# A three-mixer layer on one core: head pairs with a 64-row third product, shuffles issued by GpSimd, 13 warm-ups and a new weave

## The chip, the cores and the metric

The kernel runs on one core of a Trainium2 chip. The metric is the device time of one launch in microseconds. "TensorE" (PE), "VectorE" (DVE), "ScalarE" (ACT), "GpSimd" (POOL) and "SyncE" (SP) are the core's engines; each takes its own instructions in a fixed order and waits on semaphores. SyncE only issues transfers (DMAs); GpSimd can issue them too.

## What is computed

One layer on a sequence of T = 512 tokens with D = 1024 channels: a norm, one input projection, three mixers side by side, and an output projection with the residual.

```python
h = rmsnorm(x, norm_g[l])
proj = jnp.matmul(h, w_in[l])
(gq, gk, gv, glr, gg, su, sg, nq, nkv, ngl, ng) = jnp.split(proj, IN_SPLITS, axis=-1)
y_gla = gla_mixer(gq, gk, gv, glr, gg, ...)
y_s5 = s5_mixer(su, sg, ...)
y_nsa = nsa_mixer(nq, nkv, ngl, ng, ...)
x = x + jnp.matmul(jnp.concatenate([y_gla, y_s5, y_nsa], axis=-1), w_out[l])
```

GLA is a gated linear attention with 4 heads. S5 is a complex state-space scan in 16 groups of 64 states: chunks of 8 tokens, a scan over the 64 chunk states (xs), and a convolution inside a chunk with a table tt. NSA is an attention with 8 heads of 64 channels in two KV groups of 4 heads. It has three branches per head, mixed by gates: compressed keys, selected blocks and a window. For T = 512 the last two are both a causal softmax over all earlier tokens, each with its own keys and values:

```python
s_s = jnp.einsum('bqghd,bgqkld->bgqhkl', qb, k_g, preferred_element_type=f32)
p_s = masked_softmax(s_s.reshape(shp[:4] + (-1,)), m_s.reshape(B, G, Q_BLOCK, 1, -1)).reshape(shp)
o_s = jnp.einsum('bgqhkl,bgqkld->bqghd', p_s, v_g.astype(f32))
s_w = jnp.einsum('bqghd,bkgd->bgqhk', qb, kw, preferred_element_type=f32)
p_w = masked_softmax(s_w, m_w[None, None, :, None, :])
o_w = jnp.einsum('bgqhk,bkgd->bqghd', p_w, vw.astype(f32))
o = gb[..., 0:1] * o_c + gb[..., 1:2] * o_s + gb[..., 2:3] * o_w
```

## The kernel before

Inputs are fp32. A product that must be exact is made of three fp32r products: each operand is split into a high part hi and a low part lo = x - hi, and hi*hi, hi*lo and lo*hi are added in PSUM. ScalarE makes hi, VectorE makes lo (`load_part`, lines 224 to 226, for the weights: tiles wr, wh, wl; `split` for others). Weights of the input projection come in 12 groups of some 256 columns (su, qk, v, kv0, nq0, kv1, kv2, ng0, nq1, gg, sg, ng1), each in four parts, through a ring of six hi/lo buffers and three staging buffers wr.

The program is five streams, each a generator that yields at chosen points: p (projections), g (GLA), s (S5), n (NSA: compression and attention), o (output projection). The string ORDER (lines 43 to 48, "the weave") says which stream takes the next step. From the order in which the steps write their instructions, and from priorities, the framework sets each engine's fixed order. PSUM has eight banks: three "ps", three "pt" and two "pp"; the projections use pp.

The places that matter here:

- `start` sends nine warm-up matmuls (WARM) of 512 columns in bf16 ahead of the first real matmul, which waits for the first split of x (xh, xl). Then come the groups su and qk, the row norms and rbc. The input of S5, su, is written to DRAM (tile ud, two transfers) and read back reordered as u with eight transfers of 16 rows (line 353), all issued by SyncE.
- `gla_v` writes the values vv to DRAM (vd, line 393) and makes from them, with seven transfers, a second DRAM tile vp (line 395) in which the rows of each of seven levels stand together. `gla_intra` loads ve from vp.
- `cmp_blocks` projects kv0, scales into tm, and moves tm to aT by four transfers for each of two halves (line 943); VectorE adds positions from aT into bk (line 950).
- `s5_in` makes the tables gt, hb and kt on VectorE, writes kt and a zero block zz to DRAM (kd) and reads tt with eight transfers; `s5_scan` computes xs on VectorE. On TensorE the products "hb,xs" and "tt,u" use it.
- `attn_score` handles one head e of a head pair pr, for one block i of 128 query tokens. Keys up to the diagonal are n = 128(i+1). For i of 2 and 3 each branch has a bank of its own. The 128 rows of q hold q-hi and q-lo, those of kA[:, 0] hold k-hi twice and kA[:, 1] k-lo twice, so that two products give all four terms; the causal mask of the diagonal block is added by a third matmul of bf16 operands:

```python
mm(pb, q, kA[:, 0, br, :n], True, False)
mm(pb, q, kA[:, 1, br, :n], False, False)
mm(pb[:, n - 128:], identb, maskneg, False, True)
```

VectorE takes the row maximum, ScalarE the exponential with its sum, VectorE the reciprocal times the gate (dn), and GpSimd multiplies p by it (line 1155). `attn_out` transposes p on TensorE (line 1168), copies it out of PSUM to pT, and multiplies by the values kvr: each head's product uses 64 of the 128 columns, two heads side by side.

In the profile a matmul's tile shape stands ahead of its operands: 128*128 is the whole array, 128*64 half the columns, 64*128 half the rows.

Of the kernel before, what the change touches and what calls it, by code (L numbers as in the profile page):

```python
# [18 lines left out]
T = 512  # L19
# [16 lines left out]
for _n, _w in SMALL:  # L36
# [7 lines left out]
    "ppsgsgspppppsssspsssssgonspggsssgppgggppsgppsspgsppgppgngnsgggsnnnssspspppsggnggppppggssgggpsppggnnp"  # L44
    "gnsgpggpnpppgpgngngpggggggpgggggngggggggggggggggpppggnnnnnnpppnnnnnnnppnpnppppnnnnnnnnnpnnnppnnnnnnn"
    "nnpnnnnnnnppnnnnnnnnnnppnpppnpnnnnnnppnnnnnnnnonpppoooooooonooononnnoononnnooonnnnponnnnnnnnnnnnnnon"
    "nnoonnnnoooononnnnnooooonnnnooonnonnooooooonooooonooono"
)
WARM = 9
# [12 lines left out]
def kernel(ctx: ExitStack, tc: tile.TileContext, a: dict, out: bass.AP):  # L62
# [105 lines left out]
    identb = const.tile([128, 128], BF16, name="identb")  # L168
    maskneg = const.tile([128, 128], BF16, name="maskneg")
# [133 lines left out]
    def start():  # L303
# [29 lines left out]
        with tc.high_priority(offset=20 * BOOST):  # L333
            V.tensor_scalar(ms, ms, 1.0 / D, EPS, op0=OP.mult, op1=OP.add)
            rsqrt(rsc, ms)
            pr = bank()
            for i in range(NT):
                dg = al("dg", (128, 128))
                V.tensor_scalar(dg, ident, rsc[:, i:i + 1], None, op0=OP.mult)
                mm(pr[:, tok(i)], one, dg, True, True)  # L340
            V.tensor_copy(rbc, pr)
            ud = dram.tile([8, 256, NCH], F32, name="ud")
            for m in range(2):
                su = al("su", (128, LC, NCH))
                V.tensor_tensor(su, ps["su", m].rearrange("p (n j) -> p j n", j=LC),
                                rbc.rearrange("p (n j) -> p j n", j=LC), op=OP.mult)
                nc.sync.dma_start(out=ud[:, 128 * m:128 * m + 128].rearrange("j c n -> c j n"), in_=su)
            V.scalar_tensor_tensor(qT, ps["qk", 0], 32 ** -0.5, rbc, op0=OP.mult, op1=OP.mult)
            V.tensor_tensor(kT, ps["qk", 1], rbc, op=OP.mult)
        N["u"] = u = al("u", (128, 16, NCH), keep=True)  # L350
        for j in range(LC):
            jj = LC - 1 - j
            nc.sync.dma_start(out=u[16 * jj:16 * jj + 16], in_=ud[j].rearrange("(g c) n -> c g n", c=16))

    def consts():
# [22 lines left out]
        V.tensor_copy(identb, ident)  # L378
        V.tensor_copy(maskneg, nb)


    def gla_v():
# [9 lines left out]
        vp = dram.tile([7 * 256, 256], F32, name="vp")  # L392
# [4 lines left out]
        N["vp"] = vp  # L397
# [92 lines left out]
    def gla_intra():  # L490
        oT, vp, qT, kT = N["oT"], N["vp"], N["qT"], N["kT"]
        for lo, lv in ((-1, (0,)), (0, (1, 2)), (2, (3, 4)), (4, (5, 6))):
            with scope():
# [3 lines left out]
                for x, l in enumerate(lv):  # L497
# [6 lines left out]
                    nc.sync.dma_start(out=ve, in_=vp[l * 256:(l + 1) * 256].rearrange("(q p) e -> p q e", p=128))  # L504
# [166 lines left out]
    def s5_out_weights():  # L671
# [53 lines left out]
        nc.sync.dma_start(out=kd[0:7].rearrange("l c x -> (l c) x"), in_=zz)  # L725
# [228 lines left out]
    def cmp_mlp():  # L954
# [157 lines left out]
    def attn(gx):  # L1112
        units = [(i, pr, e) for i in (3, 2, 1, 0) for pr in range(2) for e in range(2)]
# [11 lines left out]
    def attn_score(gx, i, pr, e):  # L1125
        kA = N["kA"][gx]
        n = (i + 1) * 128
        h = gx * 4 + 2 * pr + e
        q = N[f"qA{gx}"][:, 2 * pr + e, tok(i)]
        dn = al("dn2", (128, 2), keep=True)  # L1130
        p = al("p", (128, 2, T), keep=True)
        with scope():
            nm = al("nm", (128, 2))
            if i >= 2:
                sv = []
                for br in range(2):
                    pb = bank("ps")[:, :n]
# [3 lines left out]
                    V.tensor_reduce(nm[:, br:br + 1], pb, axis=AX.X, op=OP.max, negate=True)  # L1141
                    sv.append(pb)
            else:
                pb = bank("ps")[:, :2 * n].rearrange("p (b t) -> p b t", b=2)
                mm(pb, q, kA[:, 0, :, :n], True, False)
                mm(pb, q, kA[:, 1, :, :n], False, False)
                mm(pb[:, :, n - 128:], identb, maskneg[:, None, :].to_broadcast([128, 2, 128]), False, True)
                V.tensor_reduce(nm, pb, axis=AX.X, op=OP.max, negate=True)
                sv = [pb[:, 0], pb[:, 1]]
            for br in range(2):  # L1150
                S.activation(p[:, br, :n], sv[br], AF.Exp, bias=nm[:, br:br + 1], accum_out=dn[:, br:br + 1])  # L1151
        V.reciprocal(dn, dn)
        V.tensor_tensor(dn, dn, gates[:, i, h * 3 + 1:h * 3 + 3], op=OP.mult)  # L1153
        for br in range(2):
            G.tensor_tensor(p[:, br, :n], p[:, br, :n], dn[:, br:br + 1].to_broadcast([128, n]), op=OP.mult)  # L1155
# [3 lines left out]
    def attn_out(gx, i, pr, e, live, x):  # L1159
        kvr = N["kvr"]  # L1160
        n = (i + 1) * 128
        p = live.pop(x)
        for br in range(2):
            live[e, br] = pt = al("pT", (128, T), keep=True)
            with scope():
                pb = bank("pt")
                for j in range(i + 1):
                    PE.transpose(pb[:, tok(j)], p[:, br, tok(j)], ident)  # L1168
                if cnt[0] % 2 == 0:
                    V.tensor_copy(pt[:, :n], pb[:, :n])  # L1170
                else:
                    S.activation(pt[:, :n], pb[:, :n], AF.Copy)  # L1172
# [9 lines left out]
        if i % 2:  # L1182
# [5 lines left out]
        for br in range(2):  # L1188
            for j in range(i + 1):
                for h2 in range(2):  # L1190
                    mm(o[64 * h2:64 * h2 + 64], kvr[br][:, j, 128 + gx * 64:192 + gx * 64],
                       live[h2, br][:, tok(j)], False, i % 2 == 0 and pr == 1 and br == 1 and j == i)
        for h2 in range(2):
            for br in range(2):
                fr(live.pop((h2, br)))
        yield
        if i % 2 == 0 and pr == 1:
# [21 lines left out]
def _prepare(inp):  # L1219
# [101 lines left out]
```

## Time and profile before

| | us |
|---|---|
| median of three runs | 366.1 (365.79 to 370.13) |
| profiled execution, whole time | 367.57 |
| its span from first to last instruction | 365.7 |
| TensorE busy | 341.3 (93%) |
| VectorE busy | 238.5 (65%) |
| ScalarE busy | 165.9 (45%) |
| GpSimd busy | 70.6 (19%) |
| mean granted TensorE clock | 0.977 of full |

Busy time of TensorE contains the time in which a matmul passes through the array beside the next one, so a matmul of 512 columns lasts 0.4 us though the next one starts 0.23 us after it. What a matmul costs is read from the distance of starts. Full clock is 2.4 GHz; the lower level is 1.2 GHz.

### The profile page before, as it was taken

To read this page: it belongs to the slowest core of one execution; us is meant where nothing else is said; L and a number is where in the kernel's file an instruction comes from. 1 tells how busy PE (TensorE), PEld (TensorE's weight loads), DVE (VectorE), ACT (ScalarE), POOL (GpSimd) and SP (SyncE) were. 2 spreads that over 40 slices of the span, in tenths; PEclk is the share of its full clock that TensorE was granted. 3 is DMA by queue.
4 is the path that set the end of the run, shared out by engine and by line. 5 is a ranking of instruction groups with operands and counts; after the bars stand their busy time and mean duration, and the time that the engine had idled before them with its cause. 6 is when DMAs were issued, how large, how long until landed. Compare 5 with 4: busy or idle time off the path is not lost.

```text
span 365.7 us, 6895 instructions
## 1 busy us (share of the span) xinstructions
PE 341.3 (93%) x2616; PEld 270.6 (74%) x2616; DVE 238.5 (65%) x528; ACT 165.9 (45%) x365; POOL 70.6 (19%) x92
## 2 busy tenths in 40 slices
PE   6999993989299999999999999999999898999996
PEld 3789983879177777987898777777764686777785
DVE  2847966779946467387736669647888837944332
ACT  3873541136244443453333766435876326743110
POOL 0000100000000000010100026733587117731100
PEclk9899999799789999999999999999999999999999
DMA  6996476424915355145204230001343112210122
GB/s 187 330 381 207 116 211 207 148 76 125 213 39 182 102 163 167 54 129 156 79 30 117 64 81 2 1 2 50 102 138 115 59 59 86 89 58 2 57 86 88
DMA packets 32843, 41.67 MB, mean 114 GB/s; under 512 B 7469, under 2 KB 22446, under 8 KB 32750
## 3 DMA queue, kind: packets, MB, share of 16 engines
q1 hardware_dynamic: 32810, 41.23, 37.6%
q8 instruction: 21, 0.34, 0.4%
q14 instruction: 12, 0.10, 0.1%
HBM read 35.14 MB, written 5.23 MB: 110 GB/s over the span
## 4 chain that ended last, share of the span: by engine, by line
PE 74%; DVE 11%; DMA 10%; issue 2%; SPq 1%; ACT 1%; DVEq 0%; ACTq 0%
PE pp L165 35%; PE pt L165 19%; PE ps L165 13%; PE pt L1168 5%; DMA aT<-tm 3%; DMA wor<-in_w_out_dram 2%; DMA vd<-vv 2%; DMA vp<-vd 1%; DMA w<-in_w_dram 1%; DMA xr<-in_xT_dram 1%; DVE wol L1071 1%; DVE wl L226 1%; DVE bk L950 1%; DVE h L691 1%; DVE hb L692 1%
## 5 line engine op out<-in xcount | busy, mean ns | idle before, releaser
L1155 POOL TENSOR_TENSOR p<-p,dn 128x512 f32<-128x512 f32 (+3 forms) x64 | 48.1, 775 | 41.1 <-DVE dn L1153 35.6
L165 PE MATMUL pp<-wh,xh 128*128 128x256 f32 (+2 forms) x160 | 47.6, 298 | 6.5 <-ACT qr L276 6.4
L226 DVE TENSOR_TENSOR wl<-wr,wh 128x512 fp32r<-128x512 f32 (+2 forms) x48 | 33.8, 707 | 25.7 <-ACT wh L225 25.6
L165 PE MATMUL pp<-wh,xl 128*128 128x256 f32 (+2 forms) x160 | 47.1, 295 | 0.0
L165 PE MATMUL pp<-wl,xh 128*128 128x256 f32 (+2 forms) x160 | 47.1, 295 | 0.0
L1151 ACT ACTIVATE p<-ps,nm 128x512 f32<-128x512 f32 (+3 forms) x64 | 33.2, 527 | 26.8 <-PE pt L1168 16.8
L225 ACT ACTIVATE wh<-wr 128x512 fp32r<-128x512 f32 (+2 forms) x48 | 30.4, 635 | 29.9 <-PE pp L165 11.8
L165 PEld LDWEIGHTS pp<-wh,xh 128*128 128x128 f32 x160 | 31.2, 195 | 8.7 <-ACT qr L276 6.8
L165 PE MATMUL pp<-xh,wh 128*128 128x512 f32 x80 | 32.3, 404 | 0.0
L165 PE MATMUL pp<-xh,wl 128*128 128x512 f32 x80 | 32.3, 405 | 0.0
L165 PEld LDWEIGHTS pp<-wl,xh 128*128 128x128 f32 x160 | 31.3, 195 | 1.3 <-issue 0.8
L165 PEld LDWEIGHTS pp<-wh,xl 128*128 128x128 f32 x160 | 31.2, 195 | 1.3 <-issue 0.8
L165 PE MATMUL pp<-xl,wh 128*128 128x512 f32 x80 | 32.0, 400 | 0.0
L1168 PE MATMUL pt<-ident,p 128*128 128x128 f32 x160 | 28.4, 282 | 3.3 <-DVE sc L1033 2.3
L165 PE MATMUL ps<-kA,qA 128*128 128x512 f32 (+2 forms) x96 | 29.7, 391 | 0.0
L165 PE MATMUL pt<-pT,kvr 128*64 128x128 f32 x320 | 29.4, 282 | 0.0
L1168 PEld LDWEIGHTS pt<-ident,p 128*128 128x128 f32 x160 | 18.5, 140 | 9.6 <-issue 6.0
L1141 DVE TENSOR_REDUCE nm<-ps 128x1 f32<-128x512 f32 (+1 forms) x32 | 19.4, 615 | 8.5 <-PE ps L165 8.4
L165 PEld LDWEIGHTS pt<-pT,kvr 128*64 128x64 f32 x320 | 19.9, 136 | 6.4 <-issue 3.1
L1170 DVE COPY pT<-pt 128x512 f32<-128x512 f32 (+3 forms) x32 | 15.4, 482 | 9.5 <-PE pt L1168 9.3
L1172 ACT ACTIVATE pT<-pt 128x512 f32<-128x512 f32 (+3 forms) x32 | 13.9, 434 | 16.8 <-PE pt L1168 16.8
L165 PEld LDWEIGHTS ps<-kA,qA 128*128 128x128 f32 x96 | 15.8, 191 | 3.6 <-issue 0.9
(386 smaller groups left out, 737.2 us busy)
## 6 DMA issues: line engine op xcount, KB each, us to landing
w<-in_w_dram SPq DMA_DIRECT2D x16, 256.0 KB
wor<-in_w_out_dram SPq DMA_DIRECT2D x16, 256.0 KB
xr<-in_xT_dram SPq DMA_DIRECT2D x8, 256.0 KB
xn<-in_xn_dram SPq DMA_DIRECT2D x4, 512.0 KB
wr<-in_w_kv_dram SPq DMA_DIRECT2D x8, 256.0 KB
wr<-in_w_nq_dram SPq DMA_DIRECT2D x8, 256.0 KB
wr<-in_w_ng_dram SPq DMA_DIRECT2D x8, 256.0 KB
opart<-in_xn_dram SPq DMA_DIRECT2D x4, 512.0 KB
```

Source lines behind the costliest of these rows:

```text
L165: PE.matmul(o, lhsT=l, rhs=r, start=start, stop=stop, **kw)
L225: S.activation(hs[qt][:, :, :w], r[:, :, :w], AF.Copy)
L226: V.tensor_tensor(ls[qt][:, :, :w], r[:, :, :w], hs[qt][:, :, :w].bitcast(F32), op=OP.subtract)
L691: V.tensor_tensor(t2, pj(x2), bx(cn), op=OP.mult)
L692: V.tensor_tensor(hb[c], hb[c], t2, op=OP.subtract if c == 0 else OP.add)
L950: V.tensor_tensor(b[:, :, gx * NCMP:(gx + 1) * NCMP], win, pos[:, :, None].to_broadcast([128, 16, NCMP]), op=OP.add)
L1141: V.tensor_reduce(nm[:, br:br + 1], pb, axis=AX.X, op=OP.max, negate=True)
L1151: S.activation(p[:, br, :n], sv[br], AF.Exp, bias=nm[:, br:br + 1], accum_out=dn[:, br:br + 1])
L1155: G.tensor_tensor(p[:, br, :n], p[:, br, :n], dn[:, br:br + 1].to_broadcast([128, n]), op=OP.mult)
L1168: PE.transpose(pb[:, tok(j)], p[:, br, tok(j)], ident)
L1170: V.tensor_copy(pt[:, :n], pb[:, :n])
L1172: S.activation(pt[:, :n], pb[:, :n], AF.Copy)
```

## The change

1. The weave (ORDER) is another string, and WARM is 13 instead of 9.
2. Data shuffles are issued by GpSimd, and they are fewer. ud is written with its chunk positions reversed, and w_su's columns are permuted beforehand, so that u is one transfer of 128 rows instead of eight. vd is written by GpSimd; vp is gone, and ve comes straight from vd by 14 strided loads on SyncE instead of seven. kd, tt (one transfer instead of eight), aT (eight) and vblk (eight) are issued by GpSimd.
3. Attention works on pairs of heads. A unit is a pair with one branch (i of 2 and 3) or with both (i of 0 and 1), and takes two ps banks. The mask operands are fp32r (identr, maskneg), cast by ScalarE instead of VectorE. The third product uses only the 64 rows that hold q-hi, so the term q-lo times k-lo is left out. One GpSimd multiply covers both heads; copies of pT take three or four blocks each.

```diff
@@ ORDER, WARM @@
-    "ppsgsgspppppsssspsssssgonspggsssgppgggppsgppsspgsppgppgngnsgggsnnnssspspppsggnggppppggssgggpsppggnnp"
...
+    "sssposppppppsgsgoosgssssssppnogpgsggsgspgspgssspgpppppppggngsgngnnnspgsssspggspppgpggnssppggpssgppg"
...
-WARM = 9
+WARM = 13
@@ start @@
-            ud = dram.tile([8, 256, NCH], F32, name="ud")
+            ud = dram.tile([LC, 256, NCH], F32, name="ud")
...
-                nc.sync.dma_start(out=ud[:, 128 * m:128 * m + 128].rearrange("j c n -> c j n"), in_=su)
+                nc.gpsimd.dma_start(out=ud[:, 128 * m:128 * m + 128].rearrange("j c n -> c j n"), in_=su)
...
-        for j in range(LC):
-            jj = LC - 1 - j
-            nc.sync.dma_start(out=u[16 * jj:16 * jj + 16], in_=ud[j].rearrange("(g c) n -> c g n", c=16))
+        nc.gpsimd.dma_start(out=u.rearrange("p g n -> p (g n)"), in_=ud.rearrange("j (c g) n -> (j c) (g n)", c=16))
@@ consts @@
-        V.tensor_copy(identb, ident)
-        V.tensor_copy(maskneg, nb)
+        S.activation(identr, ident, AF.Copy)
+        S.activation(maskneg, nb, AF.Copy)
@@ gla_v @@
-        nc.sync.dma_start(out=vd.rearrange("(i p) e -> p i e", p=128), in_=vv)
-        for l, s in enumerate(LEVELS):
-            nc.sync.dma_start(out=vp[l * 256:(l + 1) * 256].rearrange("(a r) e -> a r e", r=s),
-                              in_=vd.rearrange("(a two r) e -> two a r e", two=2, r=s)[0])
+        nc.gpsimd.dma_start(out=vd.rearrange("(i p) e -> p i e", p=128), in_=vv)
@@ gla_intra @@
-                    nc.sync.dma_start(out=ve, in_=vp[l * 256:(l + 1) * 256].rearrange("(q p) e -> p q e", p=128))
+                    for q in range(2):
+                        nc.sync.dma_start(out=ve[:, q], in_=vd[256 * q:256 * q + 256].rearrange(
+                            "(a two r) e -> two a r e", two=2, r=s)[0])
@@ s5_in @@
-        nc.sync.dma_start(out=kd[7:15].rearrange("l c x -> (l c) x"), in_=kt)
+        nc.gpsimd.dma_start(out=kd[7:15].rearrange("l c x -> (l c) x"), in_=kt)
...
-        for j in range(8):
-            nc.sync.dma_start(out=tt[16 * j:16 * j + 16], in_=kd[j:j + 8].rearrange("l c x -> c l x"))
+        nc.gpsimd.dma_start(out=tt, in_=bass.AP(tensor=ka.tensor, offset=ka.offset, ap=[[256, 128], [4096, 8], [1, 256]]))
@@ cmp_blocks @@
-                        nc.sync.dma_start(out=aT[64 * r:64 * r + 64, gx], in_=tm[64 * gx:64 * gx + 64, r])
+                        nc.gpsimd.dma_start(out=aT[64 * r:64 * r + 64, gx], in_=tm[64 * gx:64 * gx + 64, r])
@@ attn_score @@
-                    mm(pb, q, kA[:, 0, br, :n], True, False)
-                    mm(pb, q, kA[:, 1, br, :n], False, False)
-                    mm(pb[:, n - 128:], identb, maskneg, False, True)
+            for e in range(2):
+                mm(sv[e], q[e], kA[:, 0, b0:b0 + nb, :n], True, False)
+            for e in range(2):
+                mm(sv[e][:, :, n - 128:], identr, maskneg[:, None, :].to_broadcast([128, nb, 128]), False, False)
+            for e in range(2):
+                r = slice(64 * e, 64 * e + 64)
+                mm(sv[e], q[e][r], kA[r, 1, b0:b0 + nb, :n], False, True)
...
-            G.tensor_tensor(p[:, br, :n], p[:, br, :n], dn[:, br:br + 1].to_broadcast([128, n]), op=OP.mult)
+        G.tensor_tensor(pv, pv, dn[:, :, :, None].to_broadcast([128, 2, nb, n]), op=OP.mult)
```

How instructions move, at the places that the prediction speaks of. SyncE's queue before, from the first shuffle to the first group of aT (wr are weight parts, in_w_kv and in_w_nq those of the kv and nq groups; the rest are the shuffles named above):

```order
L347 DMA ud<-su 128x8x64 x2
L353 DMA u<-ud 16x16x64 x8
L224 DMA wr<-in_w_nq_dram 128x2x256 x3
L393 DMA vd<-vv 128x4x256
L224 DMA wr<-in_w_kv_dram 128x560
L395 DMA vp<-vd 4x16384
L395 DMA vp<-vd 8x8192
L395 DMA vp<-vd 16x4096
L395 DMA vp<-vd 32x2048
L224 DMA wr<-in_w_kv_dram 128x560
L395 DMA vp<-vd 64x1024
L395 DMA vp<-vd 128x512
```

The same stretch of SyncE's queue now, from the last part of group v on:

```order
L224 DMA wr<-in_w_v_dram 128x2x272
L365 DMA dmr<-in_dm_dram 128x1024
L224 DMA wr<-in_w_kv_dram 128x2x256 x4
L224 DMA wr<-in_w_nq_dram 128x2x256
L367 DMA w2b<-in_w2b_dram 17x128
L366 DMA dmr_579<-in_dm_dram 128x128
L224 DMA wr<-in_w_nq_dram 128x2x256 x3
L224 DMA wr<-in_w_kv_dram 128x560 x4
L224 DMA wr<-in_w_kv_dram 128x2x256
```

The shuffles no longer stand between the weight parts. They are on GpSimd's queue now, in this order (zz and xs are cleared there too):

```order
L347 DMA ud<-su 128x8x64 x2
L396 MEMSET lrT 17x512
L351 DMA u<-ud 128x1024
L390 DMA vd<-vv 128x4x256
L753 MEMSET xs 128x16
L939 DMA aT<-tm 64x256 x8
L720 MEMSET zz 112x256
L721 DMA kd<-zz 112x256
L722 DMA kd<-kt 128x256
L725 DMA tt<-kd 128x8x256
```

Each of them waits there behind the one ahead of it, and no computation of GpSimd stands between them. On TensorE, a score bank of the attention for i = 3 before (ps is the bank, qA the queries, kA the keys, pp a projection's bank):

```order
L165 MATMUL pp_3018<-xh,wh 128x512
L165 MATMUL pp_3018<-xl,wh 128x512
L165 MATMUL pp_3018<-xh,wl 128x512
L165 MATMUL ps_2199<-kA_1307,qA_942 128x512 x2
L165 LDWEIGHTS identb
L165 MATMUL ps_2199<-maskneg,identb 128x128
```

and now:

```order
L165 MATMUL pp_2815<-xh,wh 128x512
L165 MATMUL pp_2815<-xl,wh 128x512
L165 MATMUL pp_2815<-xh,wl 128x512
L165 MATMUL ps_2264<-kA_1306,qA_974 128x512
L165 MATMUL ps_2264<-maskneg,identr 128x128
L165 MATMUL ps_2264<-kA_1306,qA_974 128x512
L165 MATMUL pp_2815<-xh,wh 128x512
```

The mask stands between the bank's two products, the second of which is the one with 64 rows; the pair's other head has its own bank at another place in the order, not beside this one.

## Rows read from the trace of the kernel before

**Rows 1.** The page: busy us, share, instructions; below it tenths in 40 slices.

```profile
PE 341.3 (93%) x2616; PEld 270.6 (74%) x2616; DVE 238.5 (65%) x528; ACT 165.9 (45%) x365; POOL 70.6 (19%) x92
...
PE   6999993989299999999999999999999898999996
```

**Rows 2.** By stretches: us; busy us of PE, PEld, DVE, ACT, POOL; clock, DMA share, GB/s.

```profile
0.00:10.00 10.00, 6.85 (x17) 3.43 (x18) 2.56 (x5) 3.99 (x5) 0.56 (x8) 0.89 0.71 205
10.00:20.00 10.00, 10.00 (x42) 8.03 (x41) 7.97 (x12) 8.16 (x13) 0.00 (x0) 0.94 0.96 319
60.00:70.00 10.00, 5.34 (x24) 5.14 (x24) 4.77 (x9) 1.37 (x3) 0.00 (x0) 0.66 0.78 241
90.00:100.00 10.00, 3.29 (x33) 2.37 (x33) 10.00 (x23) 3.29 (x4) 0.00 (x0) 0.83 1.12 226
```

**Rows 3.** TensorE's waits: who waited for whom, us in total, times, longest us.

```profile
PE pp L165 <- ACT qr L276: 6.4, 2, 5.8
...
PE pt L165 <- ACT xh L292: 2.0, 1, 2.0
```

**Rows 4.** TensorE's timeline, 92 to 100 us: start, us, operation [idle before <-releaser].

```profile
96.85 0.48 PE L165 MATMUL ps<-hb,xs 64*64 64x128 f32 x2 [5.47 <-DVE rs_t L185]
...
98.79 0.48 PE L165 MATMUL ps<-hb,xs 64*64 64x128 f32 x2 [1.23 <-DVE xs L575]
```

**Rows 5.** VectorE's waits, 36 to 99 us.

```profile
DVE wl L226 <- ACT wh L225: 5.3, 2, 3.4
DVE bk L950 <- DMA aT<-tm: 3.9, 2, 2.1
```

**Rows 6.** SyncE's timeline, 38 to 76 us: start, us to issue, transfer.

```profile
42.73 4.59 SPq L353 DMA_DIRECT2D u<-ud  x8
```

**Rows 7.** The chain of waits, 30 to 110 us: start, us, what.

```profile
63.05 6.10 DMA aT<-tm
...
72.45 3.80 DMA aT<-tm
```

**Rows 8.** TensorE's timeline, from 8.3 us and from 54.8 us.

```profile
8.33 0.63 PE L165 MATMUL pt<-xl,wh 128*128 128x512 f32 x1
8.76 0.63 PE L165 MATMUL pt<-xh,wl 128*128 128x512 f32 x1
...
54.81 0.39 PE L165 MATMUL pp<-xh,wh 128*128 128x512 f32 x1
55.04 0.39 PE L165 MATMUL pp<-xl,wh 128*128 128x512 f32 x1
```

**Rows 9.** The page's groups: engine, operation, forms, count, busy us, mean ns, idle before.

```profile
L1155 POOL TENSOR_TENSOR p<-p,dn 128x512 f32<-128x512 f32 (+3 forms) x64 | 48.1, 775 | 41.1 <-DVE dn L1153 35.6
...
L226 DVE TENSOR_TENSOR wl<-wr,wh 128x512 fp32r<-128x512 f32 (+2 forms) x48 | 33.8, 707 | 25.7 <-ACT wh L225 25.6
```

**Rows 10.** TensorE's timeline at 109.25 us, transposes of ys.

```profile
109.25 0.22 PE L805 MATMUL ps<-ident,ys 64*128 64x64 f32 x1
109.26 0.22 PE L805 MATMUL pt<-ident,ys 64*128 64x64 f32 x1
```

**Rows 11.** TensorE's timeline, 310.6 to 312 us, in the attention.

```profile
310.62 0.49 PE L1168 MATMUL pt<-ident,p 128*128 128x128 f32 x3
311.04 0.43 PE L165 MATMUL pt<-pT,kvr 128*64 128x128 f32 x2
311.40 0.73 PE L165 MATMUL ps<-kA,qA 128*128 128x512 f32 x2
```

**Rows 12.** TensorE's timeline at 222 us (a mask) and at 116 us (128 columns).

```profile
222.25 0.23 PE L165 MATMUL ps<-maskneg,identb 128*128 128x128 bf16 x1
...
222.61 0.40 PE L165 MATMUL pp<-xl,wh 128*128 128x512 f32 x1
...
116.30 0.28 PE L165 MATMUL ps<-dm,Lh 128*128 128x128 f32 x1
116.42 0.28 PE L165 MATMUL ps<-dm,Ll 128*128 128x128 f32 x1
```

More of the change, by code (lines that the diff above doesn't have):

```diff
@@ L167 @@
     ident = const.tile([128, 128], F32, name="ident")
-    identb = const.tile([128, 128], BF16, name="identb")
-    maskneg = const.tile([128, 128], BF16, name="maskneg")
+    identr = const.tile([128, 128], F32R, name="identr")
+    maskneg = const.tile([128, 128], F32R, name="maskneg")
     ng = const.tile([128, NK], F32, name="ng")
@@ L1112, in attn @@
     def attn(gx):
-        units = [(i, pr, e) for i in (3, 2, 1, 0) for pr in range(2) for e in range(2)]
+        units = [(i, pr, brs) for i in (3, 2, 1, 0) for pr in range(2) for brs in (((0,), (1,)) if i >= 2 else ((0, 1),))]
         live = {}
@@ L1123, in attn, with attn_score @@
                 fr(N["kA"][gx])
-    def attn_score(gx, i, pr, e):
+    def attn_score(gx, i, pr, brs):
         kA = N["kA"][gx]
[L1127 to L1130, printed above, removed]
+        n, nb, b0 = (i + 1) * 128, len(brs), brs[0]
+        h = gx * 4 + 2 * pr
+        q = [N[f"qA{gx}"][:, 2 * pr + e, tok(i)] for e in range(2)]
+        dn = al("dn2", (128, 2, nb), keep=True)
         p = al("p", (128, 2, T), keep=True)
+        pv = p[:, :, :nb * n].rearrange("p e (b t) -> p e b t", b=nb)
@@ L1150, in attn_score @@
-            for br in range(2):
-                S.activation(p[:, br, :n], sv[br], AF.Exp, bias=nm[:, br:br + 1], accum_out=dn[:, br:br + 1])
+            nm = al("nm", (128, 2, nb))
+            sv = [bank("ps")[:, :nb * n].rearrange("p (b t) -> p b t", b=nb) for _ in range(2)]
+            for e in range(2):
+                mm(sv[e], q[e], kA[:, 0, b0:b0 + nb, :n], True, False)
+            for e in range(2):
+                mm(sv[e][:, :, n - 128:], identr, maskneg[:, None, :].to_broadcast([128, nb, 128]), False, False)
@@ L1152, in attn_score @@
+            for e in range(2):
+                r = slice(64 * e, 64 * e + 64)
+                mm(sv[e], q[e][r], kA[r, 1, b0:b0 + nb, :n], False, True)
+            for e in range(2):
+                V.tensor_reduce(nm[:, e], sv[e], axis=AX.X, op=OP.max, negate=True)
+            for e in range(2):
+                for b in range(nb):
+                    S.activation(pv[:, e, b], sv[e][:, b], AF.Exp, bias=nm[:, e, b:b + 1], accum_out=dn[:, e, b:b + 1])
         V.reciprocal(dn, dn)
-        V.tensor_tensor(dn, dn, gates[:, i, h * 3 + 1:h * 3 + 3], op=OP.mult)
@@ L1162, in attn_out @@
         p = live.pop(x)
-        for br in range(2):
-            live[e, br] = pt = al("pT", (128, T), keep=True)
+        blocks = [(e, b, j) for e in range(2) for b in range(nb) for j in range(i + 1)]
+        step = 3 if i == 2 else 4
+        pts, where = [], {}
+        for c0 in range(0, len(blocks), step):
+            pt = al("pT", (128, T), keep=True)
+            pts.append(pt)
+            part = blocks[c0:c0 + step]
             with scope():
                 pb = bank("pt")
-                for j in range(i + 1):
-                    PE.transpose(pb[:, tok(j)], p[:, br, tok(j)], ident)
+                for x_, (e, b, j) in enumerate(part):
+                    c = b * n + j * 128
+                    PE.transpose(pb[:, tok(x_)], p[:, e, c:c + 128], ident)
+                    where[e, b, j] = pt[:, tok(x_)]
+                w = len(part) * 128
@@ L1175, in attn_out @@
         fr(p)
-        if e == 0:
-            return
-        if i % 2 and pr == 0:
+        first, last = brs[0] == 0, brs[-1] == 1
+        if i % 2 and pr == 0 and first:
             live["po"] = bank("pt", keep=True)
@@ L1181, in attn_out @@
         o = po[:, pr * 256 + (i % 2) * 128:pr * 256 + (i % 2) * 128 + 128]
-        if i % 2:
+        if i % 2 and first:
             (vh, vl), (ph, pl) = N["vblk"], N["pcT"]
@@ L1187, in attn_out @@
             mm(o2, vl[:, gx, pr], ph[:, gx, c2], False, False)
-        for br in range(2):
+        for b in range(nb):
             for j in range(i + 1):
[L1190 to L1195, printed above, removed]
+                for e in range(2):
+                    mm(o[64 * e:64 * e + 64], kvr[brs[b]][:, j, 128 + gx * 64:192 + gx * 64], where[e, b, j], False,
+                       i % 2 == 0 and pr == 1 and brs[b] == 1 and j == i)
+        fr(*pts)
         yield
-        if i % 2 == 0 and pr == 1:
+        if i % 2 == 0 and pr == 1 and last:
             yield f"nsa_gate{gx}"
```

46 lines of the change are left out of this document (17 added, 29 removed).

## The prediction

> **What bounds the kernel now.** I read the page first. TensorE is busy 93% of the span, and its row in the 40 slices shows where it is not: the seventh slice has 3 tenths, the eleventh 2, and after that nearly every slice is full [rows 1]. So the program has two stages: up to about 100 us TensorE waits for other engines, afterwards it is itself the bound. The table by stretches says the same: TensorE has 5.34 of 10 us in 60 to 70 and 3.29 in 90 to 100, where VectorE is busy for 10.00 of 10 [rows 2]. From this follows how each part is priced: work added to TensorE after 100 us counts in full, work taken from the other engines there counts nothing, and before 100 us only what brings the last awaited instruction forward counts.
>
> TensorE's own waits name that instruction: 6.4 us for the evacuation qr, 5.8 of it in one piece [rows 3], then 5.5 + 1.2 us for what S5 computes on VectorE; the second half of hb,xs starts at 98.79, released by xs [rows 4]. The wait for qr doesn't set the end of the stage, because TensorE catches up and then stands before xs anyway. VectorE's waits from 36.5 to 99 us are 5.3 us for wh and 3.9 for aT [rows 5]; wh waits for weights, and both come through the SyncE queue. There the eight u<-ud alone take 4.59 us [rows 6], and weight loads stand behind them. The chain of waits goes through the landing of aT, 6.10 and 3.80 us [rows 7].
>
> **The change part by part.** All sums are made against the profiled execution: 367.57 us, of which the span is 365.7, and 1.9 lie around it. That execution is 1.5 us above the median of 366.1; I carry the difference over to the median.
>
> *Warm-up, 13 matmuls instead of 9.* The first real matmul waits 2.0 us for xh [rows 3], and soon after it matmuls of 512 columns start 0.43 us apart instead of 0.23 [rows 8]; the granted clock is 0.89 in the first 10 us and 0.94 in the second [rows 2], so a piece of them ran at the lower level of 1.2 GHz. (1 - 0.89) + (1 - 0.94), of 10 us each, is 1.7 us of lost clock. Four more warm-ups lie in the idle 2 us and cost nothing there; the clock can then stay up. I take -1.6, with the ends 0 and -1.7.
>
> *The shuffles leave SyncE.* In the order SyncE now goes from the constants straight on to the weights of kv0, nq and kv1, with no transfer between them that waits for a computed tile. So the 5.3 us for wh can go. The 3.9 us for aT can shrink, but the new transfers stand one behind another on GpSimd: aT behind vd<-vv, and kd and tt behind aT. No DMA issued by GpSimd is in the trace of before, so its price is bounded: from nothing (GpSimd is busy 0.00 us in 60 to 70 and in 90 to 100 [rows 2], so issue lies beside other work) up to the landings of [rows 7], 4 to 6 us a second time for a dependent step. By the order VectorE meets aT 16 rows after the first tm and 7 rows after the second. A wide row of the split or of S5 takes some 0.7 us (33.8 us for 48 wl [rows 9]), and about half are wide: some 6 and 4 us. Against landings of 3.80 to 6.10 that leaves 0 to 2 us of wait. So of the 9.2 us some 1.5 stay: -7.7. The ends are 0 (the GpSimd queue costs what it saves) and -9.2. What is late next is VectorE itself: its work up to xs is dense then, and the first matmul that waits for the whole of xs comes at about 91 instead of 98.8. TensorE reaches it before that; 475 matmuls stand ahead of it in the order where 471 did (4 are warm-ups). So TensorE idles there as before and drops to the lower clock level there as before (0.83 in [rows 2]); I credit neither.
>
> Something speaks against that term: VectorE is busy in much of these stretches, 10.00 of 10 in the last of them [rows 2]. The Trainium skill (SBUF — State Buffer, "SBUF: two separate sides") warns that a transfer issued from GpSimd has its descriptors written by GpSimd's cores, which are locked out while VectorE runs an operation in its two-port mode; no run shown so far can confirm or deny it. What late GpSimd transfers would do here is rival D.
>
> *Third product with 64 rows.* It takes a tile of 64*128 instead of 128*128 and streams the same 512 columns. It gains only if the two heads' products, in different row halves, run at once: two transposes of ys do, at 109.25 and 109.26 [rows 10]. But in the order of the changed program they never stand side by side: every bank has its first product, its mask and its third product, and then comes other work. So no columns are saved, and the change of tile shape is paid. Its price [rows 11]: three transposes of 0.27 take 0.49 together, so they start 0.11 apart and the last at 310.84; the first 128*64 product comes at 311.04, 0.20 later. Two of those (0.43 together) put the second at 311.20, and the product kA follows at 311.40, again 0.20 later. The two kA products take 0.73, and a product of 512 columns lasts 0.40 [rows 12], so they start 0.33 apart instead of 0.23. So about 0.094 us for a change of shape, and 0.05 to 0.1 more after a return. Counted over the TensorE order, changes of shape go from 163 to 230: 67 x 0.094 = 6.3 us, and half of them are returns, 33 x 0.075 = 2.5. Sum +8.8. Ends: 0 (nothing is paid where the stationary operand is that of the first product), and 13.8 (all 48 third products alone, at 0.094 + 0.094 + 0.1). The rule of the Trainium skill (TensorEngine Tiling (Array Packing), "Key Properties") that a change of tiling mode drains the engine speaks against this edit too; it has no figure, the rows give one.
>
> *Mask in fp32r.* A bf16 mask at 222.25 and the product behind it take 0.36 together, 0.13 more than the product's 0.23; fp32r products of 128 columns start 0.12 apart [rows 12]. So 48 masks cost 0, between -1 and +1.
>
> *Fewer instructions on the other engines.* GpSimd's 64 multiplies of p take 48.1 us [rows 9]; 24 larger ones move the same elements. After 100 us TensorE is the bound, so fewer instructions elsewhere gain 0. The cost if cover is short: a pair holds two of three score banks, and p of both heads comes after one multiply twice as long, 0.8 us later by the mean there. Over 24 units a tenth of that not covered is 2 us, all of it 18.
>
> **Sum.** -1.6 - 7.7 + 8.8 + 0 = -0.5 us: 367.57 becomes 367.1, and against the median 365.6. About 2% (7.3 us) is what a measurement of this kernel can tell from no change, so this is no change.
>
> **The rivals.**
>
> A is the forecast, 365.6. In a weaker form the change doesn't do what it says at the front: S5 is late for its own sake, and only 3 us come back: 366.1 - 1.6 - 3 + 8.8 = 370.3, also within 2%.
>
> B, changes of shape are hidden. A third product has the stationary operand of the first one and follows a short mask; if it pays hardly any drain, the term is 1 instead of 8.8: 366.1 - 1.6 - 7.7 + 1 = 357.8. Against it: [rows 11] show the price in both directions, products of 512 columns too.
>
> C, the front closes: the new weave gives TensorE work while it waits. Its waits there are 6.4 + 5.5 + 1.2 = 13.1 [rows 3, 4], and with them goes the low clock behind the first (0.66 of 10 us, 3.4 us lost, of which I take 2). 366.1 - 1.6 - 13.1 - 2 + 8.8 = 358.2. Against it: as many matmuls as before stand ahead of the wait for xs.
>
> D, the GpSimd queue becomes the wait. VectorE stands in order at bk, and behind bk are gt, the scans and xs. If aT comes some 10 us after tm instead of 4 to 6, the second bk waits 5 us more, and with u and tt behind too the whole 7.7 us are gone: 366.1 - 1.6 + 8.8 = 373.3; each us more adds one, and with the upper end of the drains it is 378. It decides from the point where xs isn't earlier than now. For it: a serial queue of 16 transfers up to tt, with waits in it. Against it: GpSimd has nothing else to do there.
>
> **How the numbers follow.** A 0.38, its weaker form 0.07, B 0.20, C 0.14, D 0.21 (0.20 of it beyond 2%). Faster by over 2%: B and C, 0.34. Within 2%: 0.38 + 0.07 + 0.01 = 0.46. Slower: 0.20. The likeliest case gives 365.6; its own range is 361 (drains at about 4) to 371 (drains at 13.8). The whole range takes in B and C at its low end, and D with dearer drains at its high end: 355 to 376.
>
> **What would show it.** Right: a granted clock near 1 in the first 10 us; wh no longer late; the long row of hb,xs on TensorE starting at about 91; VectorE's waits for aT at 1.5 us; lone 64*128 products with 0.2 us or more around each pair of changes. Wrong: hb,xs at 98 or later (then D); TensorE busy through 80 to 95 us (then C); 64-row products that stand no further apart than the others (then B).

## The result and the profile after

The changed kernel takes 369.03 us (median of 20 runs, 366.52 to 371.45), the kernel before 367.77 (20 runs, 364.51 to 371.11). The ratio is 1.006, 95% interval 1.0032 to 1.0087: slower by 0.6%, some 2.2 us. The medians are over all runs and the ratio leaves out a slower state that some executions fall into, so the medians don't divide to it. The forecast was 0.5 us faster. The time lies within the range and within the 2%, but the sign was wrong. The single runs of either kernel spread over 5 to 7 us, so the profiled executions (before 367.57, after 369.08) are compared by their parts, and the kernels by ratios.

The page after, as in [rows 1] (busy us, share, instructions; below it tenths in 40 slices):

```profile
PE 349.5 (95%) x2620; PEld 274.4 (75%) x2620; DVE 238.7 (65%) x500; ACT 167.0 (45%) x357; POOL 74.8 (20%) x75
...
PE   8999898991999999999999999999999999999996
```

The dip of the seventh slice is gone, that before xs has moved from slice eleven to ten. TensorE is busy 8.2 us longer. The table by stretches, as in [rows 2] (us; busy us of PE, PEld, DVE, ACT, POOL; clock, DMA share, GB/s):

```profile
0.00:10.00 10.00, 8.20 (x26) 4.11 (x27) 3.07 (x5) 4.13 (x6) 0.56 (x8) 1.00 0.74 206
10.00:20.00 10.00, 10.00 (x45) 8.12 (x44) 7.37 (x11) 8.31 (x14) 0.00 (x0) 1.00 1.01 340
...
60.00:70.00 10.00, 10.00 (x88) 9.63 (x89) 9.97 (x13) 2.64 (x6) 2.95 (x6) 1.00 0.27 69
...
80.00:90.00 10.00, 3.67 (x26) 2.74 (x24) 10.00 (x21) 4.42 (x5) 1.49 (x2) 0.71 0.42 124
90.00:100.00 10.00, 8.85 (x97) 6.53 (x99) 4.53 (x12) 3.11 (x4) 0.00 (x0) 0.61 0.46 159
```

The front came out as drawn: full clock in the first 20 us, TensorE full in 60 to 70, VectorE dense there and up to 90, and TensorE waiting in 80 to 90. TensorE's timeline from 80 to 101 us, as in [rows 4], has

```profile
88.52 0.69 PE L165 MATMUL ps<-hb,xs 64*64 64x128 f32 x4 [4.56 <-DVE rs_t L185]
90.46 0.69 PE L165 MATMUL ps<-hb,xs 64*64 64x128 f32 x4 [1.24 <-DVE xs L571]
...
94.89 0.70 PE L165 MATMUL pt<-tt,u 128*64 128x128 f32 x4
```

The product that waits for xs starts at 90.46 instead of 98.79: 8.3 us earlier. Behind it stands something new: the table tt was issued at 88.76 and lands 5.6 us later, so the first product with it comes only at 94.89. The transposes of ys, before and now, are the point up to which the gain can be followed:

```profile
108.83 0.52 PE L805 MATMUL pt<-ident,ys 64*128 64x64 f32 x5
```

```profile
101.79 0.71 PE L801 MATMUL pt<-ident,ys 64*128 64x64 f32 x8
```

The gain is 7.0 us there. One profile doesn't fix it to the us. The kernel before with 64 rows (below) has the same order ahead of xs as the kernel before, and there the last operation of xs starts at 95.7 instead of 98.0; in the changed kernel and its three versions with another third product or mask it starts between 88.2 and 89.7. VectorE's waits from 36 to 99 us, as in [rows 5]:

```profile
DVE dec L443 <- ACT ex L433: 2.5, 1, 2.5
DVE wl L226 <- ACT wh L225: 1.7, 3, 0.7
```

The wait for aT is gone, that for wh is 1.7 instead of 5.3. So 7 us arrive at the transposes of ys, and at the end the program takes 1.6 more than before (spans 367.3 and 365.7): behind ys it takes 265.5 us instead of 256.9. The attention stands there. Three banks of it, on TensorE, where [rows 11] had other work:

```profile
233.10 0.81 PE L165 MATMUL ps<-kA,qA 64*128 64x384 f32 x2
233.75 0.22 PE L165 MATMUL ps<-maskneg,identr 128*128 128x128 f32 x1
233.91 0.81 PE L165 MATMUL ps<-kA,qA 64*128 64x384 f32 x2
234.55 0.22 PE L165 MATMUL ps<-maskneg,identr 128*128 128x128 f32 x1
```

A row "x2" is the third product of one bank and the first of the next. From one mask to the next are 0.80 us. All starts of score products and masks, each counted up to the next instruction's start with idle time left out, sum to 27.0 us in the trace of before and to 39.0 in this one: +12.0. The value products pT,kvr, in which the pairs stand closer together, sum to 24.9 instead of 26.7: -1.7.

### The profile page after: what moved, and what is told of

Read it like the earlier page. It is cut to its first block, busy times and chain, and to the rows that moved or that the text cites. A ratio compares the mean times of both kernels' runs of the same rounds, so it can differ in the third digit from the quotient of the medians.

```text
span 367.3 us, 6790 instructions
## 1 busy us (share of the span) xinstructions
PE 349.5 (95%) x2620; PEld 274.4 (75%) x2620; DVE 238.7 (65%) x500; ACT 167.0 (45%) x357; POOL 74.8 (20%) x75
## 4 chain that ended last, share of the span: by engine, by line
PE 73%; DMA 12%; DVE 10%; issue 2%; ACT 1%; SPq 1%; ACTq 0%; DVEq 0%
PE pp L165 37%; PE pt L165 16%; PE ps L165 13%; PE pt L1165 5%; DMA xr<-in_xT_dram 4%; DMA wr<-in_w_v_dram 3%; DMA wr<-in_w_kv_dram 3%; DMA wor<-in_w_out_dram 2%; DVE wl L226 1%; DMA dmr<-in_dm_dram 1%; DVE hb L688 1%; DVE ml L1084 1%; ACT wh L225 1%; DVE cm L570 0%; DVE cm L567 0%
## 5 line engine op out<-in xcount | busy, mean ns | idle before, releaser
L1146 POOL TENSOR_TENSOR p<-p,dn 128x1024 f32<-128x1024 f32 (+2 forms) x24 | 39.2, 1636 | 54.2 <-DVE dn L1145 32.7
L165 PE MATMUL pp<-wh,xh 128*128 128x256 f32 (+2 forms) x160 | 46.1, 289 | 3.2 <-ACT qr L276 1.7
L165 PE MATMUL ps<-kA,qA 128*128 128x512 f32 (+3 forms) x96 | 40.8, 440 | 0.0
L1140 DVE TENSOR_REDUCE nm<-ps 128x1 f32<-128x512 f32 (+3 forms) x48 | 28.5, 598 | 14.0 <-PE ps L165 13.5
L165 PE MATMUL pt<-pT,kvr 128*64 128x128 f32 x320 | 27.2, 281 | 1.4 <-ACT pT L1171 1.4
L165 PEld LDWEIGHTS ps<-kA,qA 128*128 128x128 f32 (+1 forms) x96 | 17.7, 186 | 11.6 <-issue 6.5
L1165 PE MATMUL pt<-ident,p 128*128 128x128 f32 x160 | 25.1, 284 | 0.0
L1171 ACT ACTIVATE pT<-pt 128x512 f32<-128x512 f32 (+1 forms) x22 | 12.2, 556 | 22.6 <-PE pt L1165 22.5
L1165 PEld LDWEIGHTS pt<-ident,p 128*128 128x128 f32 x160 | 17.0, 140 | 5.8 <-issue 5.2
L1169 DVE COPY pT<-pt 128x512 f32<-128x512 f32 (+1 forms) x22 | 14.0, 638 | 8.1 <-PE pt L1165 7.8
```

The costliest lines, as they stand in the source:

```text
L165: PE.matmul(o, lhsT=l, rhs=r, start=start, stop=stop, **kw)
L1140: V.tensor_reduce(nm[:, e], sv[e], axis=AX.X, op=OP.max, negate=True)
L1146: G.tensor_tensor(pv, pv, dn[:, :, :, None].to_broadcast([128, 2, nb, n]), op=OP.mult)
L1165: PE.transpose(pb[:, tok(x_)], p[:, e, c:c + 128], ident)
L1169: V.tensor_copy(pt[:, :w], pb[:, :w])
L1171: S.activation(pt[:, :w], pb[:, :w], AF.Copy)
```

## The experiments

"Ratio" is to the kernel before, measured together with the run. The first four were measured together.

**128 rows in the third product** (the changed kernel, else as it is).

```diff
-                r = slice(64 * e, 64 * e + 64)
-                mm(sv[e], q[e][r], kA[r, 1, b0:b0 + nb, :n], False, True)
+                mm(sv[e], q[e], kA[:, 1, b0:b0 + nb, :n], False, True)
```

> The changed kernel with a third product over all 128 rows again (so it keeps the 128*128 tile), all else kept. Theory 1, the drains: the order loses 80 changes of tile shape (230 to 150), 80 x 0.094 plus 40 returns x 0.075 = 10.5 us, so about 358.5 us, ratio to the kernel before 0.975. Theory 2, the mask in fp32r is what is dear (its starts sum to 7.9 us against 4.6): only the kA share goes, some 7 to 8 us, 361. Theory 3, the pairs hold banks too long and tile shapes cost nothing: 0 to -2 us, 367 to 369.

356.57 us, ratio 0.9655 (0.9592 to 0.9719). This version is 3.45% faster than the kernel before. Against the changed kernel's 1.006 that is 14.9 us; the like pair with bf16 masks, measured together (369.52 and 358.22, below), differs by 11.3. TensorE's order is the same row by row in all of these but for the edited products. Theory 1 holds; its price (10.5) was somewhat low. The same kind of place in its trace:

```profile
229.68 0.57 PE L165 MATMUL ps<-kA,qA 128*128 128x384 f32 x2
230.09 0.22 PE L165 MATMUL ps<-maskneg,identr 128*128 128x128 f32 x1
230.14 0.57 PE L165 MATMUL ps<-kA,qA 128*128 128x384 f32 x2
230.55 0.22 PE L165 MATMUL ps<-maskneg,identr 128*128 128x128 f32 x1
```

From mask to mask are 0.46 us instead of 0.80, with 384 columns streamed twice in both and twice the rows in one of the products. The starts of scores and masks sum to 27.9 us instead of 39.0, which is 0.23 for each of the 48 third products on average, and behind the transposes of ys the program takes 253.0 us instead of 265.5.

**A bf16 mask in the changed kernel.**

```diff
-    identr = const.tile([128, 128], F32R, name="identr")
-    maskneg = const.tile([128, 128], F32R, name="maskneg")
+    identr = const.tile([128, 128], BF16, name="identr")
+    maskneg = const.tile([128, 128], BF16, name="maskneg")
```

> The changed kernel with its mask operands in bf16 again, the third product still over 64 rows. Theory 1, the drains: the time behind the mask is the drain before the 64-row product, not the mask, so 0 within 1 us, 368 to 370 us. Theory 2, the mask's type is dear: -3.3 us, about 366.

369.52 us, ratio 1.0022 (0.9974 to 1.0071), against 1.006 (1.0032 to 1.0087): no difference that can be told. Theory 2 falls: the time from a mask to the next start is 0.16 us here in the median, 0.15 with the fp32r mask, and 0.06 where 128 rows follow, so it is the change of shape ahead of the 64-row product.

**Both.**

> The changed kernel with 128 rows in the third product and a bf16 mask. Theory 1: the same as with 128 rows alone, about 358.5 us, within 1 us of it; the front gain of 8 us is then seen whole against the kernel before. Theory 2: 3.3 us below 128 rows alone. Theory 3: 366 to 369.

358.22 us, ratio 0.9702 (0.9617 to 0.9787): the same as with 128 rows alone, by the intervals.

**9 warm-ups in the changed kernel** (WARM = 9).

> The changed kernel with 9 warm-ups instead of 13 (the order of TensorE changes in some 77 rows of 1600, too). Theory A: the warm-up gains nothing, because VectorE, not TensorE, sets the end of the front; xs comes when it did, time within 1 us of the changed kernel's 369. Theory B, as predicted: the lost clock of the first 20 us comes back in full, +1.6 us. In both the clock of the first 10 us falls to about 0.89.

371.48 us, ratio 1.0053 (1.0015 to 1.0091), against 1.006: by the ratios no difference. Against the kernel with a bf16 mask and 13 warm-ups, which was measured together with it (369.52), it is 2.0 us slower, near theory B's 1.6. Its trace, by stretches, TensorE's first products and the last operation of xs:

```profile
0.00:10.00 10.00, 6.30 (x14) 3.02 (x15) 2.77 (x5) 3.96 (x6) 0.57 (x8) 1.00 0.73 201
```

```profile
8.31 0.63 PE L165 MATMUL ps<-xh,wh 128*128 128x512 f32 x1
8.74 0.63 PE L165 MATMUL pt<-xh,wh 128*128 128x512 f32 x1
```

```profile
94.17 0.68 DVE L571 TENSOR_TENSOR xs<-cm,cm 128x504 f32<-128x504 f32 x1
```

The table has a granted clock of 1.00 where the expectation had 0.89, but the products up to 12.6 us start 0.43 us apart and last 0.63, as in [rows 8], which is the lower level. So here the table misses what the starts show. The starts go with the warm-ups in every trace: in the five with nine (this one, the kernel before, and three runs below) 6 to 10 products start 0.43 apart there, in the eight with 13 and no products added at most one does. And xs is 4.5 us later than in the changed kernel (94.17 instead of 89.72), so theory A's condition fails. As TensorE's order differs too, up to 77 us, the run doesn't tell what the four warm-ups are worth by themselves.

**64 rows in the kernel before**, nothing else changed.

```diff
-                    mm(pb, q, kA[:, 1, br, :n], False, False)
+                    mm(pb, q[64 * e:64 * e + 64], kA[64 * e:64 * e + 64, 1, br, :n], False, False)
```

> The kernel before, with nothing changed but its third products, which go over 64 rows (q-lo times k-lo is left out). The order of TensorE stays the same row by row; changes of tile shape go from 163 to 259. Drain theory: 96 x 0.094 + 48 x 0.075 = 12.6 us by the prediction's prices, or 14 to 15 us by what the changed kernel gave back with 128 rows; ratio 1.034 to 1.04. Rival (the pairs' banks, not the tile shape, cost the time): ratio 1, within 0.003.

378.56 us, ratio 1.0246 (1.0185 to 1.0306): +9 us. The rival falls, since here are no pairs. The drain theory's 12.6 to 15 us were too much for the whole time. Its page:

```profile
PE 352.6 (94%) x2616; PEld 272.6 (73%) x2616; DVE 238.9 (64%) x528; ACT 166.5 (45%) x365; POOL 69.8 (19%) x92
```

TensorE is busy 352.6 of 373.4 us instead of 341.3 of 365.7: 11.3 us more work and 3.6 us less idle. Of the idle time 1.9 us went ahead of the transposes of ys, where no score product stands (the first starts at 181.6) and where this execution was 2.8 us earlier without any edit there. The other 1.7 went after 210 us, where part of the longer products can lie in waits that TensorE had anyway. Behind ys the program takes 10.5 us more (267.4 instead of 256.9).

**The price by itself**: 144 products in fp32r behind the warm-ups.

```diff
+            for _ in range(12):
+                for e in range(2):
+                    mm(sb[e], hw, fz, True, False)
+                for e in range(2):
+                    mm(sb[e], hw[R[e]], fz[R[e]], False, True)
...
```

> The changed kernel with 128 rows and, behind its warm-ups, 144 extra products of 512 columns in fp32r that no result uses (its time is longer by them). Three blocks of twelve cycles, a cycle being two first products and two third products on two banks: (a) the two 64-row products side by side, (b) each alone behind its first product, (c) over 128 rows. By the prices of the prediction: (c) 4 x 0.23 = 0.92 us a cycle; (b) 0.92 + 4 x 0.094 + 2 x 0.075 = 1.45; (a) if row halves run at once: 3 x 0.23 + 2 x 0.094 + 0.075 = 0.95, so the pair, even side by side, gains nothing over 128 rows; if they don't: 1.18.

Its timeline, first block (a), side by side:

```profile
6.73 0.50 PE L165 MATMUL pt<-fz 128*128 128x512 f32 x1
7.08 0.39 PE L165 MATMUL pp<-fz 128*128 128x512 f32 x1
7.40 0.49 PE L165 MATMUL pt<-fz 64*128 64x512 f32 x1
7.40 0.49 PE L165 MATMUL pp<-fz 64*128 64x512 f32 x1
7.82 0.50 PE L165 MATMUL pt<-fz 128*128 128x512 f32 x1
```

and the same view of block (b), alone, and of block (c), 128 rows:

```profile
19.98 0.50 PE L165 MATMUL pp<-fz 64*128 64x512 f32 x1
20.41 0.92 PE L165 MATMUL pt<-fz 128*128 128x512 f32 x2
21.26 0.93 PE L165 MATMUL pp<-fz 128*128 128x512 f32 x2
...
45.89 0.40 PE L165 MATMUL pp<-fz 128*128 128x512 f32 x1
46.12 0.40 PE L165 MATMUL pt<-fz 128*128 128x512 f32 x1
46.36 0.39 PE L165 MATMUL pp<-fz 128*128 128x512 f32 x1
```

In (c) products start 0.23 apart: 0.93 us a cycle, at full clock. In (a) both halves start together, so they do run at once, and still the cycle is 1.09 (6.73 to 7.82), more than (c). In (b) every start is 0.43 after the last one: 1.72 a cycle. A product lasts 0.50 us there, where at the lower clock level it lasts 0.63 [rows 8], so this is the change of shape and not the clock. So a change of shape between products of 512 columns costs 0.20 us, in either direction, and a lone product 0.40. From 35.5 us on, still in (b), the starts are 0.72 apart, and the table has

```profile
30.00:40.00 10.00, 10.00 (x20) 4.16 (x20) 5.01 (x28) 1.32 (x2) 0.00 (x0) 0.77 0.11 41
```

The clock fell to its lower level though TensorE was busy for 10.00 of 10 us with these alternating products.

**Everything but the attention** (weave, warm-ups and shuffles as changed; single heads, 128 rows, bf16 mask).

> Everything of the change but the attention (so 128-row products, single heads and a bf16 mask as before; new weave, 13 warm-ups, new shuffles). If pairs as such gain nothing: like the changed kernel with 128 rows, ratio 0.965 to 0.975. If the pairs themselves bring something (fewer changes of shape in the value products, 1.7 us, and fewer, larger instructions): 2 to 4 us slower than that, ratio 0.975 to 0.98.

370.95 us, ratio 1.0083 (1.0049 to 1.0117): neither of the two, and 4.3 points above the pairs with 128 rows. TensorE's busy time from 210 to 350 us shows where, for this kernel and then for the one with pairs and 128 rows:

```profile
210.00:350.00 140.00, 132.70 (x878) 99.04 (x876) 91.50 (x197) 67.06 (x193) 64.16 (x77) 0.98 0.19 57
```

```profile
210.00:350.00 140.00, 137.64 (x931) 109.87 (x930) 95.90 (x177) 66.63 (x186) 56.08 (x37) 1.00 0.20 61
```

TensorE idles 7.3 us there with single heads and 2.4 with pairs, and its granted clock is 0.98 instead of 1.00. The weave string is made for the steps of pairs, so this doesn't tell what pairs gain under a string of their own.

**The new shuffles alone, and the new weave alone, in the kernel before.**

> The kernel before with the new shuffles alone (issued by GpSimd, fewer, ve straight from vd); weave, warm-ups and attention as before. Theory 1: SyncE's queue was the cause of VectorE's 9.2 us of waits, so xs comes some 8 us earlier and the time falls by 6 to 8 us, ratio 0.978 to 0.984. Theory 2: the new weave, not the queue, brought the front forward; then 0 to -2 us, ratio 0.995 to 1.

> The kernel before with the new weave string alone. Theory 1: 0 within 2 us, since the SyncE queue still holds VectorE up (the attention has more steps than the string was made for, so the tail may lose a little). Theory 2: -4 to -8 us.

The shuffles alone: 368.84 us, ratio 1.0045 (1.0003 to 1.0088). xs is finished 5.4 us earlier (its last operation starts at 92.6 instead of 98.0; 3.1 earlier than the 95.7 of the run with 64 rows), and nothing of it reaches the end: from 210 to 350 us TensorE idles 6.6 us instead of 3.4, waiting for p, pcT and others. The weave alone: 382.68 us, ratio 1.0401 (1.0329 to 1.0473), with xs 3.3 us earlier, but the transposes of ys at 112.6 instead of 108.8. In both runs both theories missed: xs is earlier in either, by more than or near the 2.3 us that it moves by itself, and the rest of the order gives it back.

**All shuffles back on SyncE, then a part of them** (the changed kernel with 128 rows; still the fewer transfers).

```diff
-                nc.gpsimd.dma_start(...)
+                nc.sync.dma_start(...)
```

> The changed kernel with 128 rows in the third product, and its shuffles issued by SyncE again (still the fewer ones, vp gone). Theory 1: what counts is that weight loads wait behind shuffles in SyncE's order, so wh is late again and 4 to 8 us of the front gain are lost, ratio 0.977 to 0.987. Theory 2: their number counts, not the queue; then within 2 us of 0.9655.

369.38 us, ratio 1.0028 (0.9981 to 1.0076). That looks like a gain of 13 us by GpSimd's queue, but its trace has xs at 90.1 us, hardly later than the 89.2 with GpSimd. Row by row, the order of TensorE had changed behind xs. So the next two part the shuffles ahead of xs from those behind it.

> The changed kernel with 128 rows, and ud, u, vd and aT issued by SyncE again, between the weight parts; kd, tt and vblk stay on GpSimd. TensorE's order differs in 10 rows only, all ahead of xs. Theory 1, the prediction's (the shuffles in SyncE's queue hold the weights up): xs comes 3 us or more later than 89.9 and the ratio to the kernel before is 0.974 or more. Theory 2 (fewer transfers and the new weave are enough, whichever queue issues them): xs within 1 us, ratio 0.962 to 0.970.

ud, u, vd and aT on SyncE: 356.44 us, ratio 0.9655 (0.9618 to 0.9692), xs at 89.0. It is the same as with GpSimd. For these transfers the queue makes no difference under the new weave; theory 2 holds.

> The changed kernel with 128 rows, and only kd, tt and vblk issued by SyncE. In the order TensorE now finishes bank ps of hb,xs and tt,u ahead of bank pt, so that their 64*64 tiles no longer stand side by side. Order theory: the 13 us that all shuffles on SyncE cost come from here, ratio 0.995 to 1.006, first transposes of ys at about 110 instead of 102. Queue theory: the loss came from the other transfers, ratio 0.963 to 0.972.

kd, tt and vblk on SyncE: 370.34 us, ratio 0.9992 (0.9933 to 1.0051). The whole 13 us are here (13.9 against the run with the first transfers on SyncE, measured together), though the first tt,u starts at 93.5 us, 0.9 earlier than with GpSimd. Its timeline:

```profile
93.75 0.42 PE L165 MATMUL ps<-tt,u 128*64 128x128 f32 x2
94.11 1.12 PE L165 MATMUL ps<-hb,xs 64*64 64x128 f32 x8
95.16 0.69 PE L165 MATMUL ps<-tt,u 128*64 128x128 f32 x4
95.78 1.12 PE L165 MATMUL ps<-hb,xs 64*64 64x128 f32 x8
```

and with GpSimd:

```profile
95.44 0.48 PE L165 MATMUL pt<-hb,xs 64*64 64x128 f32 x2
95.45 0.48 PE L165 MATMUL ps<-hb,xs 64*64 64x128 f32 x2
95.71 0.42 PE L165 MATMUL pt<-hb,xs 64*64 64x128 f32 x2
95.72 0.42 PE L165 MATMUL ps<-hb,xs 64*64 64x128 f32 x2
```

With GpSimd, tiles of the two banks alternate, and pairs of ps and pt start 0.01 apart. With SyncE one bank is done ahead of the other, and nothing runs beside it. At the same lower clock eight products hb,xs then take 1.05 us (94.11 to 95.16), where with alternating banks sixteen take 1.06 (95.44 to 96.50). The larger part is the clock. By stretches, with SyncE and then with GpSimd:

```profile
100.00:110.00 10.00, 10.00 (x69) 7.01 (x69) 2.59 (x4) 2.28 (x4) 0.00 (x0) 0.50 0.01 2
110.00:120.00 10.00, 9.91 (x44) 7.82 (x45) 3.16 (x9) 1.79 (x3) 0.00 (x0) 0.50 0.08 26
```

```profile
100.00:110.00 10.00, 9.70 (x80) 7.37 (x77) 6.38 (x14) 4.57 (x7) 0.00 (x0) 1.00 0.18 54
110.00:120.00 10.00, 10.00 (x73) 8.03 (x73) 4.63 (x6) 4.84 (x10) 0.00 (x0) 1.00 0.48 161
```

From 80 to 130 us the lost clock (one less the granted share, times the stretch) sums to 18.8 us with SyncE and to 6.9 with GpSimd. The difference of 11.9 lies almost wholly where TensorE is busy throughout, and is most of the 14.0 us between the two spans (368.7 and 354.7). With all shuffles on SyncE, in the same order, it is 12.0. So the order and the low clock come together in both runs; what holds the clock down there no run shows. The transposes of ys start at 111.2 instead of 101.7.

## Why the prediction was wrong, step by step

**Where the sum failed.** In the two profiled executions the time up to the transposes of ys fell by 7.0 us, where -1.6 and -7.7, together -9.3, were forecast, and behind them it rose by 8.6, where +8.8 was. So the sign was lost in the front. That the part behind it came out is luck: the third product was dearer than priced, and a gain that the prediction put at 0 made up for it.

**The step that failed first: the price of the 64-row product.** The mechanism stood in the prediction (the products are not side by side, and the change of shape is paid), its size did not. The +8.8 is a net count, in which the value products' fewer changes are already taken off. For the third products alone the same prices give 10.5 (80 changes, as in the expectation for 128 rows). Measured were 11.3 (369.52 to 358.22, together, with bf16 masks) and 14.9 (by the two ratios, with fp32r masks); the starts give +12.0, or +10.3 with the value products' -1.7. The error is in how the price was read from [rows 11]: "0.094 us for a change of shape, and 0.05 to 0.1 more after a return". The second half was counted on returns only. The test by itself shows 0.20 us in both directions with 512 columns, so 0.40 for a lone product; in the attention, with its short mask ahead, it was 0.34 where it stood alone (0.80 less 0.46), and 0.23 on average. That the products come beside each other would not have helped either: 1.09 against 0.93 us a cycle. Rival B is refuted.

**The second: the front, -9.3, was carried whole to the end.** At xs 8.3 came, and 1.3 of it went behind xs, where tt lands 5.6 us after its issue (the clock, 0.61 in 90 to 100, was not told apart from it). The prediction named a late tt only under rival D. For the shuffles the size, -7.7, is near what came, known to some 2 us; the reason is wrong. "So the 5.3 us for wh can go" came true in the main (1.7 are left), and the wait for aT went. But it is not because the shuffles left SyncE: with ud, u, vd and aT issued by SyncE between the weight parts, the time is the same. What is left of the change there is that the transfers are fewer, and the new weave; the new shuffles alone brought xs forward by 5.4 us, the weave alone by 3.3. Rival D is refuted with it: the eight aT landed in 2.5 us on GpSimd (median, 1.8 to 4.3) where [rows 7] had 3.8 to 6.1, u in 5.4. The lockout that the Trainium skill (SBUF — State Buffer, "SBUF: two separate sides") warns of is not to be seen here, while VectorE is busy for 9.97 of 10 us; whether its operations there were of the two-port kind no run shows. Rival C is refuted: TensorE waited 4.6 + 1.2 us before xs.

**Warm-up, -1.6: not settled.** The starts 0.43 us apart are gone, and TensorE's products of the row norm came 2.3 us earlier (33.1 instead of 35.5). But VectorE copied rbc at 37.40 instead of 36.55, since weights and S5 tables stood ahead of it in its order, and xs took its time from there. By the prediction's own rule, that ahead of 100 us only the last awaited instruction counts, the term needed a reason why it should reach xs, and it had none. It isn't shown to be 0 either: with 9 warm-ups in the changed kernel rbc waited 1.3 us for TensorE and came at 38.19, xs came 4.5 us later, and the time was 2.0 us above that of the run measured with it; but the order differs there.

**Mask, 0: right**, by the bf16 mask put back.

**Fewer instructions elsewhere, 0: too little.** With 128 rows the program behind the transposes of ys takes 253.0 us instead of 256.9, so 3.9 are gained there that no term had. In the kernels with an early front, single heads leave TensorE idle for 6.6 and 7.3 us from 210 to 350 us, the pairs for 1.4 to 2.5, and the value products change shape less often (-1.7). The 3.9 are likely these, which was not tried by itself.

**The sum.** By the runs all but the rows is worth -12.7 (ratio 0.9655), and the rows cost the 14.9 that the two ratios differ by, which is +2.2 (with 11.3 for the rows it would be -1.4, so the sign hangs on the ratios). Gain and loss were both larger than forecast, and nearly cancel. What stays open is how much of the 12.7 is the pairs' own, as the weave string fits only their steps, and why the new shuffles alone give back all they gain.

## What to carry to other kernels

A product over half the rows doesn't stream fewer columns. Before an edit changes the array's tile shape, count the changes in the order that is really issued, and price each from rows in which both neighbours are as long as yours, on the way in as well as on the way out. And when a part is undone in a scheduled kernel, compare the order of every engine first: moving a few transfers to another queue cost 13 us here, with TensorE's products in another order and its clock at the lower level for longer. Before a gain on one engine is booked, name the instruction by which it reaches the last one to arrive. And read the clock from the distance of starts too, not from the granted share alone.

## What the runs showed of the hardware

Two fp32r products of 512 columns in different row halves start within 0.01 us of each other, and a change between whole and half arrays costs 0.20 us a time (measured with lone products), so a cycle of two whole products and such a pair takes longer than one of four whole ones (1.09 and 0.93 us). A mask of 128 columns costs the same in bf16 and in fp32r within the measurement (1.0022 and 1.006 with 64 rows, 0.9702 and 0.9655 with 128). Tiles of 64*64 on two banks ran side by side where they alternate in the order (sixteen in 1.06 us) and not where one bank was done ahead of the other (eight in 1.05). The granted clock can be low while TensorE is busy: 0.50 from 100 to 120 us in the run with kd, tt and vblk on SyncE, 0.77 from 30 to 40 in the test of the price. And it can be listed as 1.00 where the starts, 0.43 us apart, show the lower level (the run with 9 warm-ups, first 12.6 us).
